# Hybrid diffusion trunk: weight splits emitted ahead in the scheduler's order, two steps of the RWKV units offered later to TensorE

## The chip, the cores and the metric

One core of a Trainium2 chip. The time is device microseconds of one execution of the program, the median of several runs; a profile of one execution stands beside it.

## What is computed

Two layers of one trunk over 512 latent tokens and 256 context tokens, 1024 wide, everything in 32-bit floats. Each layer is a half-step SwiGLU, token mixing, and another half-step SwiGLU, each behind a modulated RMS norm. Layer 0 mixes with eight heads of global attention beside eight heads of a bidirectional RWKV-7 recurrence; layer 1 with windowed attention.

```python
for l in range(DEPTH):
    x = x + 0.5 * m_lat[:, 2] * swiglu(modulate(rms_norm(x), m_lat[:, 0], m_lat[:, 1]), ffn_in[l, 0], ffn_out[l, 0])
    ctx = ctx + 0.5 * m_ctx[2] * swiglu(modulate(rms_norm(ctx), m_ctx[0], m_ctx[1]), ffn_in[l, 0], ffn_out[l, 0])
    ...
    o_lat, o_ctx = even_mixer(h_lat, h_ctx, ...) if l % 2 == 0 else odd_mixer(h_lat, h_ctx, ...)
    x = x + m_lat[:, 5] * o_lat
    x = x + 0.5 * m_lat[:, 8] * swiglu(modulate(rms_norm(x), m_lat[:, 6], m_lat[:, 7]), ffn_in[l, 1], ffn_out[l, 1])
    ...
return rms_norm(x, final_gain)

def step(S, inp):                     # the recurrence, one token, both directions
    r, w, k, v, kk, a = inp
    S = (S * w[:, :, None, :] - jnp.einsum('bhvk,bhk->bhv', S, kk)[..., None] * (kk * a)[:, :, None, :]
         + v[..., None] * k[:, :, None, :])
    return S, jnp.einsum('bhvk,bhk->bhv', S, r)
```

## The kernel before

**Dense products.** Each product with a weight is made in three matmuls of rounded 32-bit operands (`mm3`, L138 to L140): upper half of the weight times upper half of the activation (hi), upper times lower (lo), lower times upper. `weights` (L119 on) loads a 128x512 piece of a weight into `raw` by a DMA of SyncE (four buffers) and has `split` make `whi` on ScalarE (L116) and `wlo` on VectorE (L117), three buffers each. L138 and L139 read `whi`, L140 reads `wlo`. Four blocks of 128 columns come out of one piece. `d`, `g`, `c`, `y`, `s` are accumulation banks: two each of `d` and `g`, one of `c` and `y`, and one double bank `s` for attention.

**The even mixer** (some 600 to 1760 us) runs several generators merged into one order of TensorE. `dense` makes the projections of the context (256 columns a matmul) and of the latents (512), then the context's output product and its feed-forwards. `recurrence` is the chain of the RWKV units, twelve of them: four pairs of heads of the context (units 0 to 3), then four of the latents in two halves (4 to 11). `attention` makes the softmax tiles: scores L666, maximum L668 on VectorE, exponential L671 on ScalarE, transposes L610, values L624. `queued` takes what comes behind a projection: the norm of a query or key tile (`a_prepare2`, sums L380, reciprocal root by L333 on ScalarE and L334 on GpSimd, copy L389 on ScalarE, spread L392).

**What sets the order on TensorE.** `merge` (L175 on) keeps a clock in microseconds of TensorE. A generator yields a pair: how long its matmuls take, by which the clock goes on, and how long its next step's inputs take to be ready; it is offered again when the clock has passed 1.32 times the second number (L206). Of those offered the first in rank goes, or `dense` when it is owed a share (0.42, later 0.52 of the work). TensorE works through that order as it stands.

**What sets it on the other engines.** There a scheduler places the instructions by a priority, which is the place in the program less a boost. `merge` traces the steps of the recurrence under `high_priority(120)`; nothing else has a boost.

**A unit of the recurrence.** `rwkv_inverse` begins with sixteen matmuls for the four blocks of each direction d (L785): eight for d = 0 into two `g` banks, masked by two VectorE instructions (L787), then eight for d = 1 into two `g` banks again. Between the two stands a yield (L788). Later steps invert a triangular block in five levels (L822, L840). `rwkv_blocks` then goes through four blocks: L888 and L893 read the state, L899 multiplies by the inverse, VectorE (L900) and ScalarE (L901) copy the result, and L905 and L916 use it for the next state and the output; the yield between (L902) says 0.35 and 0.8.

Of the kernel before, what the change touches and what calls it, by code (L numbers as in the profile page):

```python
# [42 lines left out]
def flat(x):  # L43
    return x.rearrange("p a t -> p (a t)")
# [10 lines left out]
def fold(x):  # L55
    return x.rearrange("p (d t) -> p d t", d=2)
# [14 lines left out]
class Kernel:  # L71
# [47 lines left out]
    def weights(self, src, n, s):  # L119

        nc, pool = self.nc, s.wp
        out = []
        for c in range(0, n, 512):
            w = min(512, n - c)
            if self.early:
                raw = self.early.pop(0)
            else:
                raw = self.t(pool, [P, 512], "raw", bufs=4 if pool is self.wp else 3)
                nc.sync.dma_start(raw[:, :w], src[:, c : c + w])
            hi = self.t(pool, [P, 512], "whi", F32R, bufs=3)  # L130
            lo = self.t(pool, [P, 512], "wlo", F32R, bufs=3)
            self.split(raw[:, :w], hi[:, :w], lo[:, :w])
            out += [(hi[:, i : i + P], lo[:, i : i + P]) for i in range(0, w, P)]
        return out

# [39 lines left out]
    def merge(self, *gens, keep=None):  # L175


        gens += (keep,) if keep else ()
        self.parts, self.clock = [[rank, 0.0, gen] for rank, gen in enumerate(gens)], 0.0
        owed = 0.0  # L180
        with self.tc.manual_schedule(engines={mybir.EngineType.PE}):
            while self.parts:
                self.pause = keep is not None and len(self.parts) == 1
                ready = [p for p in self.parts if p[1] <= self.clock]
                if not ready:
                    self.clock = min(p[1] for p in self.parts)
                    continue
                p = min(ready, key=lambda p: p[0])
                if keep is not None and owed > 0:
                    p = next((q for q in ready if q[2] is keep), p)  # L190
                try:

                    with self.tc.high_priority(120) if p[2] in self.urgent else nullcontext():
                        step = next(p[2])
                except StopIteration:
                    self.parts.remove(p)
                    continue
                if step == "rest":
                    if len(self.parts) == 1:
                        break  # L200
                elif step is None:
                    p[1] = self.clock + 0.2
                else:
                    self.clock += step[0]
                    owed = min(owed + self.share * step[0], 2) - (step[0] if p[2] is keep else 0)
                    p[1] = self.clock + step[1] * 1.32  # L206
        self.parts, self.pause = None, False
# [562 lines left out]
    def rwkv_inverse(self, u):  # L770
# [9 lines left out]
        for d in (0, 1):  # L780
            mask = self.gmask[:, d].unsqueeze(1).to_broadcast([P, 4, P])
            pss = [self.bank("g") for _ in (0, 1)]
            for c in range(4):
                for e, q, _ in HALVES:
                    mm(pss[e][:, c * P : (c + 1) * P], flat(BK[q, 4 * d + c]), flat(A[q, 4 * d + c]), start=True, stop=True)  # L785
            for e, ps in enumerate(pss):
                tt(X[e][:, 4 * d : 4 * d + 4].rearrange("p c a t -> p c (a t)"), ps.rearrange("p (c n) -> p c n", n=P), mask, op=ALU.mult)  # L787
            yield 1.2, 0.6 * d  # L788


        ds = (slice(0, 4), slice(4, 8))
# [66 lines left out]
    def rwkv_blocks(self, u, S, Sout):  # L858


        nc, rp, W, A, X, PT, UV, tok = self.nc, self.rp, u.W, u.A, u.X, u.PT, u.UV, u.tok
        tt, mm, act = nc.vector.tensor_tensor, nc.tensor.matmul, nc.scalar.activation

        def decayed(s, n):

            if s is None:
                return None
            o = self.t(rp, [P, 2, 64], "SW", bufs=2)
            f, b = 64 + 66 * n, BS + 1 + 66 * (3 - n)
            nc.gpsimd.tensor_tensor(o, s, W[:, f : b + 1 : b - f].unsqueeze(2).to_broadcast([P, 2, 64]), op=ALU.mult)  # L870
            return o

        yb = self.bank("y")

        def y(d, c, q):
            return yb[q, c * 64 : c * 64 + 64]

        SW = decayed(S, 0)
        for n in range(4):
            pr = slice(n, 8 - n, 7 - 2 * n)  # L880
            bl = ((0, n), (1, 7 - n))
            cp = self.bank("c")
            if S is None:
                R = u.LV[:, pr]
            else:
                for d, c in bl:
                    for e, q, _ in HALVES:
                        mm(cp[q, 64 * d : 64 * d + 64], A[q, c, 0], S[q, d], start=True, stop=True)  # L888


                for d, c in bl:
                    for e, q, _ in HALVES:
                        mm(y(d, c, q), S[q, d], A[q, c, 1], start=n == d == 0, stop=False, skip_group_check=True)  # L893
                R = self.t(rp, [P, 2, 64], "R", bufs=2)
                tt(R, fold(cp[:, :128]), u.LV[:, pr], op=ALU.add)
                yield 0.75, 0.3
            for d, c in bl:
                for e, q, _ in HALVES:
                    mm(cp[q, 128 + 64 * d : 192 + 64 * d], PT[q, c], R[q, d], start=True, stop=True)  # L899
            nc.vector.tensor_copy(UV[:64, pr, 0], fold(cp[:64, 128:256]))  # L900
            act(UV[64:, pr, 1], fold(cp[64:, 128:256]), AF.Copy)  # L901
            yield 0.35, 0.8  # L902
            for d, c in bl:
                for e, q, _ in HALVES:
                    mm(cp[q, 256 + 64 * d : 320 + 64 * d], tok[:, c, e], UV[:, c, e], start=True, stop=True)  # L905
            Sn = Sout if n == 3 else self.t(rp, [P, 2, 64], "S", bufs=2)
            if Sn is not None:
                if SW is None:
                    nc.vector.tensor_copy(Sn, fold(cp[:, 256:384]))
                else:  # L910
                    tt(Sn, fold(cp[:, 256:384]), SW, op=ALU.add)
                if n < 3:
                    SW = decayed(Sn, n + 1)
            for d, c in bl:
                for e, q, _ in HALVES:
                    mm(y(d, c, q), UV[:, c, e], X[e][:, c, 1], start=S is None, stop=S is None or n == 3 and d == 1,  # L916
                       skip_group_check=S is not None)
            S = Sn
            yield 0.75, 0.2
        return yb  # L920
# [669 lines left out]
```

## Time and profile before

| what | before |
|---|---|
| median of 3 runs | 3248.78 us (3246.76 to 3249.76) |
| profiled execution, its own time | 3245.93 us |
| its span, first to last instruction | 3244.1 us |
| TensorE busy | 3072.4 us (95%) |
| VectorE busy | 2012.8 us (62%) |
| ScalarE busy | 1246.8 us (38%) |
| mean granted clock of TensorE | 0.981 |

Busy time of TensorE counts pipelined matmuls as they overlap, so a busy TensorE may still stream below its rate; a stall shows more plainly as idle time of the weight loads (PEld), each of which stands at the head of a matmul. The stages in order of time: first feed-forward of both streams to some 620 us, the even mixer to 1760, the feed-forwards of the latents with what is left of the context's work to 2500, the odd mixer to 2860, the last feed-forward.

### The profile page before, as it was taken

How to read it: one execution, taken by the hardware profiler on the slowest of the kernel's cores; microseconds unless marked ns; L12 is line 12 of the kernel's file. 1: busy time of each engine (PE TensorE's matmuls, PEld its weight loads, DVE VectorE, ACT ScalarE, POOL GpSimd, SP SyncE). 2: the span in 40 equal slices, each digit the busy share in tenths (PEclk: the TensorE clock that was granted, in tenths of full speed). 3: DMA queues.
4: the chain of work that ended last, by engine and by line, in shares of the span. 5: the costliest groups of instructions: out<-in, count | busy, mean ns of one | idle time of the engine just before them, and what ended most of it. 6: DMA issues, size and time to landing. Idle time of an engine off the chain costs nothing. (4 is left out here: it accounts for less than half of the span.)

```text
span 3244.1 us, 57779 instructions
## 1 busy us (share of the span) xinstructions
PE 3072.4 (95%) x22910; PEld 2623.1 (81%) x22910; DVE 2012.8 (62%) x3956; ACT 1246.8 (38%) x2595; POOL 303.7 (9%) x333
## 2 busy tenths in 40 slices
PE   5999999999997999999999999999999988999998
PEld 3888888887776789897888888888888867778887
DVE  7999973676665776767765444454344667754434
ACT  4222212544343444444444323343223456632322
POOL 3000000111124110102001000010000132010001
PEclk9999999999998999999999999999999999999999
DMA  6677672531111123332334333333333320023332
GB/s 229 206 215 216 211 257 61 169 101 58 43 43 54 33 88 99 95 100 74 101 128 134 107 96 97 96 116 97 97 96 95 113 75 24 27 81 97 96 97 88
DMA packets 174431, 349.59 MB, mean 108 GB/s; under 512 B 19408, under 2 KB 30544, under 8 KB 173776
## 3 DMA queue, kind: packets, MB, share of 16 engines
q1 hardware_dynamic: 169984, 340.86, 34.0%
q10 hardware_dynamic: 4176, 5.05, 0.5%
q8 instruction: 179, 2.93, 0.4%
q14 instruction: 92, 0.75, 0.1%
HBM read 340.59 MB, written 5.24 MB: 107 GB/s over the span
## 5 line engine op out<-in xcount | busy, mean ns | idle before, releaser
L116 ACT ACTIVATE whi<-raw 128x512 fp32r<-128x512 f32 (+1 forms) x996 | 615.4, 619 | 1359.5 <-PE d L139 502.0
L117 DVE TENSOR_TENSOR wlo<-raw,whi 128x512 fp32r<-128x512 f32 (+1 forms) x996 | 681.2, 686 | 683.3 <-ACT whi L116 667.2
L138 PE MATMUL d<-hL,whi 128*128 128x512 f32 x944 | 381.9, 405 | 3.2 <-ACT hL L404 2.6
L139 PE MATMUL d<-hL,whi 128*128 128x512 f32 x944 | 374.7, 397 | 2.3 <-DVE hL L405 2.2
L140 PE MATMUL d<-hL,wlo 128*128 128x512 f32 x944 | 371.9, 394 | 1.4 <-DVE wlo L117 1.4
L138 PE MATMUL d<-hC,whi 128*128 128x256 f32 x968 | 299.4, 309 | 7.6 <-ACT whi L116 4.5
L140 PE MATMUL d<-hC,wlo 128*128 128x256 f32 x968 | 278.4, 288 | 7.1 <-DVE wlo L117 6.7
L284 DVE SCALAR_TENSOR_TENSOR junk<-qL,cb 128x1024 bf16<-128x1024 f32 x224 | 273.3, 1220 | 11.6 <-DMA qL<-wmod 9.1
L139 PE MATMUL d<-hC,whi 128*128 128x256 f32 x968 | 277.2, 286 | 0.0
L140 PEld LDWEIGHTS d<-hL,wlo 128*128 128x128 f32 x944 | 179.8, 190 | 43.0 <-DVE wlo L117 2.6
L138 PEld LDWEIGHTS d<-hC,whi 128*128 128x128 f32 x968 | 188.5, 195 | 22.0 <-issue 6.9
L138 PEld LDWEIGHTS d<-hL,whi 128*128 128x128 f32 x944 | 180.3, 191 | 28.1 <-ACT hL L404 3.4
L139 PEld LDWEIGHTS d<-hL,whi 128*128 128x128 f32 x944 | 180.5, 191 | 24.2 <-DVE hL L405 3.6
L140 PEld LDWEIGHTS d<-hC,wlo 128*128 128x128 f32 x968 | 188.7, 195 | 10.2 <-DVE wlo L117 9.8
L139 PEld LDWEIGHTS d<-hC,whi 128*128 128x128 f32 x968 | 189.1, 195 | 0.5
L138 PE MATMUL d<-pL,whi 128*128 128x512 f32 x416 | 162.8, 391 | 0.0
L139 PE MATMUL d<-pL,whi 128*128 128x512 f32 x416 | 162.2, 390 | 0.0
L140 PE MATMUL d<-pL,wlo 128*128 128x512 f32 x416 | 162.0, 390 | 0.0
L138 PE MATMUL g<-hL,whi 128*128 128x512 f32 x384 | 149.4, 389 | 0.0
L139 PE MATMUL g<-hL,whi 128*128 128x512 f32 x384 | 149.4, 389 | 0.0
L140 PE MATMUL g<-hL,wlo 128*128 128x512 f32 x384 | 149.4, 389 | 0.0
L354 POOL TENSOR_TENSOR acc<-acc,sq 128x512 f32<-128x512 f32 x30 | 39.0, 1300 | 933.8 <-issue 710.6
(533 smaller groups left out, 6602.2 us busy)
## 6 DMA issues: line engine op xcount, KB each, us to landing
raw<-ffn_in SPq DMA_DIRECT2D x528, 256.0 KB, 2.9
qL<-wmod SPq DMA_DIRECT2D x132, 512.0 KB, 4.2
raw<-ffn_out SPq DMA_DIRECT2D x248, 256.0 KB, 2.7
raw<-even_in SPq DMA_DIRECT2D x84, 256.0 KB, 2.6
raw<-even_out SPq DMA_DIRECT2D x32, 256.0 KB, 2.6
raw<-odd_in SPq DMA_DIRECT2D x32, 256.0 KB, 2.8
raw<-ffn_out SPq DMA_DIRECT2D x56, 128.0 KB, 2.1
pL<-wmod SPq DMA_DIRECT2D x8, 512.0 KB, 8.8
```

The lines of the kernel that those rows point to most:

```text
L116: self.nc.scalar.activation(hi, src, AF.Copy)
L117: (eng or self.nc.vector).tensor_tensor(lo, src, hi.bitcast(F32), op=ALU.subtract)
L138: mm(out, w[0], mh, start=first, stop=False)
L139: mm(out, w[0], ml, start=False, stop=False)
L140: mm(out, w[1], mh, start=False, stop=last)
L284: nc.vector.scalar_tensor_tensor(self.t(self.fp, [P, D], "junk", bf), w, 0.5, self.cb[:, v], op0=ALU.mult, op1=ALU.mult, accum_out=out)
L354: eng.tensor_tensor(s.sq[0], s.sq[0], x, op=ALU.add)
```

## The change

Three things. The two instructions of each weight split are traced under a boost of 60, and the boost of the recurrence is raised from 120 to 160. The step of direction 1 in the first step of a unit is offered 1.2 x 1.32 us after the end of direction 0's matmuls, where it was offered at once. The step from L899 to L905 is offered 1.05 x 1.32 us after the clock where it was 0.8 x 1.32.

```diff
@@ weights
-            self.split(raw[:, :w], hi[:, :w], lo[:, :w])
+
+            with self.tc.high_priority(60):
+                self.split(raw[:, :w], hi[:, :w], lo[:, :w])
@@ merge
-                    with self.tc.high_priority(120) if p[2] in self.urgent else nullcontext():
+                    with self.tc.high_priority(160) if p[2] in self.urgent else nullcontext():
                         step = next(p[2])
@@ rwkv_inverse
-            yield 1.2, 0.6 * d
+
+            yield 1.2, 0.6 if d else 1.2
@@ rwkv_blocks
             act(UV[64:, pr, 1], fold(cp[64:, 128:256]), AF.Copy)
-            yield 0.35, 0.8
+            yield 0.35, 1.05
```

No instruction is added or removed. The lines of the changed kernel are two higher from the splits on (L138 is L140) and three higher behind L788 (L905 is L908).

TensorE, unit 0 (context), its first step; `pL` are the unit's own tiles, the rows of `hC` are dense matmuls. Before:

```order
L785 MATMUL g<-pL 128x128 x16
L138 MATMUL d<-hC,whi 128x256
L139 MATMUL d<-hC,whi 128x256
L140 MATMUL d<-hC,wlo 128x256
...
L806 MATMUL g<-ident,pL 64x64 x8
```

And now:

```order
L787 MATMUL g<-pL 128x128 x8
L140 MATMUL d<-hC,whi 128x256
L141 MATMUL d<-hC,whi 128x256
L142 MATMUL d<-hC,wlo 128x256
...
L787 MATMUL g<-pL 128x128 x8
```

The sixteen are parted in two eights, and 18 dense matmuls stand between them (three of these rows six times). Units 1, 4, 5 and 10 are parted in the same way.

TensorE, unit 0, its third and fourth block (L899 writes bank `c`, L905 needs the copy of it; `s` rows are the norm of a key tile). Before:

```order
L899 MATMUL c<-R,pL 64x64 x4
L905 MATMUL c<-pL 64x64 x4
L916 MATMUL y<-pL 64x64 x4
L392 MATMUL s<-ident,sq 128x128 x2
L888 MATMUL c<-S,pL 64x64 x4
L893 MATMUL y<-pL,S 64x64 x4
L899 MATMUL c<-R,pL 64x64 x4
L138 MATMUL d<-hC,whi 128x256
...
L905 MATMUL c<-pL 64x64 x4
```

And now, the end of the third block and the fourth:

```order
L382 MATMUL s<-bones,sq 128x2 x2
L908 MATMUL c<-pL 64x64 x4
L919 MATMUL y<-pL 64x64 x4
L140 MATMUL d<-hC,whi 128x256
...
L891 MATMUL c<-S,pL 64x64 x4
L896 MATMUL y<-pL,S 64x64 x4
L902 MATMUL c<-R,pL 64x64 x4
L394 MATMUL s<-ident,sq 128x128 x2
L908 MATMUL c<-pL 64x64 x4
```

The third block, bare before, now has twelve dense matmuls and a pair of sums ahead of L908; the fourth, which had twelve, has one transposing pair.

VectorE at the norm of the latents, beside the projections of the context (L403 and L405 modulate the latents, L685 and L686 shift a projected feature). Before:

```order
L117 TENSOR_TENSOR wlo<-raw,whi 128x512
L405 SCALAR_TENSOR_TENSOR hL<-pL,mod0L,hL 128x512
L685 SCALAR_TENSOR_TENSOR gC<-d,par,gC 128x255
L405 SCALAR_TENSOR_TENSOR hL<-pL,mod0L,hL 128x512
L686 SCALAR_TENSOR_TENSOR gC<-d,par,gC 128x255
L117 TENSOR_TENSOR wlo<-raw,whi 128x512
```

And now:

```order
L407 SCALAR_TENSOR_TENSOR hL<-pL,mod0L,hL 128x512
L117 TENSOR_TENSOR wlo<-raw,whi 128x512
L407 SCALAR_TENSOR_TENSOR hL<-pL,mod0L,hL 128x512
L117 TENSOR_TENSOR wlo<-raw,whi 128x512 x2
L687 SCALAR_TENSOR_TENSOR gC<-d,par,gC 128x255
L405 SCALAR_TENSOR_TENSOR pL<-qL,mod0L,s 128x512
L688 SCALAR_TENSOR_TENSOR gC<-d,par,gC 128x255
L117 TENSOR_TENSOR wlo<-raw,whi 128x512
```

Splits have moved ahead of modulations of the latents and of shifts of features.

## Rows read from the trace of the kernel before

**Rows 1.** The page's busy time: us, share of the span, instructions.

```profile
PE 3072.4 (95%) x22910; PEld 2623.1 (81%) x22910; DVE 2012.8 (62%) x3956; ACT 1246.8 (38%) x2595; POOL 303.7 (9%) x333
```

**Rows 2.** Windows: us; busy PE, PEld, DVE, ACT, POOL (count); granted clock, DMA, GB/s.

```profile
100.00:500.00 400.00, 398.84 (x2285) 349.92 (x2283) 369.83 (x682) 87.29 (x157) 0.00 (x0) 1.00 0.70 216
620.00:1000.00 380.00, 345.13 (x3674) 283.61 (x3672) 248.48 (x538) 166.32 (x393) 64.43 (x82) 0.97 0.23 72
1000.00:1020.00 20.00, 12.96 (x62) 10.22 (x62) 5.20 (x16) 4.53 (x14) 12.05 (x16) 0.57 0.00 0
1020.00:1760.00 740.00, 704.14 (x8603) 633.45 (x8604) 514.65 (x1062) 338.80 (x714) 102.52 (x111) 0.98 0.30 91
1760.00:2500.00 740.00, 736.31 (x3450) 618.18 (x3449) 333.44 (x513) 246.38 (x409) 8.77 (x7) 1.00 0.34 101
```

**Rows 3.** Waits of weight loads, 620 to 1760 us: total us, times, longest.

```profile
PEld s L610 <- ACT pr L671: 9.8, 11, 2.2
PEld d L140 <- DVE wlo L117: 8.5, 10, 2.0
```

**Rows 4.** Line L787 (masking), who waited for it: us, times.

```profile
  PEld g L785: 9.8, 14
```

**Rows 5.** Line L901 (copy), who waited for it: us, times.

```profile
  PEld c L905: 12.4, 17
```

**Rows 6.** Timeline at 1516 us: start, us, engine, line, operation [idle before].

```profile
1516.06 1.16 PE L785 MATMUL g<-hL 64*128 64x128 f32 x16
...
1517.69 1.28 DVE L787 TENSOR_TENSOR hL<-g,gmask 128x512 f32<-128x512 f32 x2
...
1518.42 1.75 PE L785 MATMUL g<-hL 64*128 64x128 f32 x16 [1.20 <-DVE hL L787]
```

**Rows 7.** Timeline at 1158 us, TensorE, behind eight covered matmuls of L785.

```profile
1158.16 0.38 PE L138 MATMUL d<-hC,whi 128*128 128x256 f32 x1
1158.38 0.28 PE L139 MATMUL d<-hC,whi 128*128 128x256 f32 x1
1158.50 0.28 PE L140 MATMUL d<-hC,wlo 128*128 128x256 f32 x1
```

**Rows 8.** Timeline at 1129 us, a block step without cover.

```profile
1128.79 0.45 PE L899 MATMUL c<-R,hL 64*64 64x64 f32 x8
...
1130.10 0.27 ACT L901 ACTIVATE hL<-c 64x128 f32<-64x128 f32 x1 [0.22 <-DVE hL L900]
1130.42 0.31 PEld L905 LDWEIGHTS c<-hL 128*64 128x64 f32 x8 [1.32 <-ACT hL L901]
```

**Rows 9.** Timeline at 648 us, a lower half behind a modulation.

```profile
647.66 0.74 DVE L405 SCALAR_TENSOR_TENSOR hL<-pL,mod0L,hL 128x512 fp32r<-128x512 f32 x1
...
648.16 0.28 PE L139 MATMUL d<-hC,whi 128*128 128x256 f32 x1
...
648.71 0.68 DVE L117 TENSOR_TENSOR wlo<-raw,whi 128x512 fp32r<-128x512 f32 x1
...
649.45 0.38 PE L140 MATMUL d<-hC,wlo 128*128 128x256 f32 x1 [1.01 <-DVE wlo L117]
```

**Rows 10.** The page's groups: count, busy us, mean ns, idle us before.

```profile
L116 ACT ACTIVATE whi<-raw 128x512 fp32r<-128x512 f32 (+1 forms) x996 | 615.4, 619 | 1359.5 <-PE d L139 502.0
L117 DVE TENSOR_TENSOR wlo<-raw,whi 128x512 fp32r<-128x512 f32 (+1 forms) x996 | 681.2, 686 | 683.3 <-ACT whi L116 667.2
```

**Rows 11.** Windows of 5 us in the first feed-forward, at either clock.

```profile
58.00:63.00 5.00, 4.89 (x16) 4.17 (x16) 5.00 (x13) 2.01 (x4) 0.00 (x0) 0.50 0.01 3
80.00:85.00 5.00, 5.00 (x30) 4.40 (x29) 3.86 (x10) 1.43 (x3) 0.00 (x0) 1.00 0.55 178
```

**Rows 12.** Waits of weight loads, 980 to 1020 us, the norms of query tiles.

```profile
PEld s L392 <- ACT sq L389: 5.1, 3, 2.1
```

**Rows 13.** Waits of weight loads, 625 to 655 us.

```profile
PEld d L140 <- DVE wlo L117: 4.1, 6, 1.2
```

## The prediction

> **What bounds the kernel now.** TensorE is busy for 3072.4 of 3244.1 us, VectorE for 2012.8 [rows 1], so the first question is where TensorE is not streaming. The windows by stage answer it [rows 2]: from 1760 to 2500 us it is busy for 736.31 of 740 at a granted clock of 1.00, and there a new order of the same matmuls cannot win anything. From 620 to 1760 us, the stage of the even mixer, it is busy for 345.13 + 12.96 + 704.14 = 1062.2 of 1140 us, so some 78 us are idle, and the clock is 0.97, 0.57 and 0.98. Nearly all that the change reorders on TensorE, and so nearly all that it can move, lies in these 1140 us; the number of instructions is the same on every engine.
>
> Then I read who is waited for there. A weight load stands at the head of each matmul and starts only when its data is there, so its idle time is the plainest measure of a stall. Three of the groups are what the three edits touch. The 64-row matmuls of the first step of an RWKV unit (L785) wait 9.8 us in 14 waits for the masking L787 [rows 4]. The state update of a block (L905) waits 12.4 us in 17 waits for the copy L901 [rows 5]. The third matmul of a split product (L140) waits 8.5 us in 10 waits for the lower half of a weight split, L117 [rows 3]. Together that is 30.7 us, under 1% of the span, and it bounds the direct gain.
>
> **The masking step, now offered later for direction 0.** Both directions need two banks "g", and there are two. Where their sixteen matmuls stand in one piece, the second eight wait until VectorE has masked both banks. In the unit at 1516 us the first eight end at 1516.06 + 1.16 = 1517.22, the two maskings end at 1517.69 + 1.28 = 1518.97, and the second eight begin only at 1518.42 and are stretched over 1.75 us instead of 1.16 [rows 6]. So a cover of about 1.75 us is wanted. The order shows what stands between now: in unit 0 nothing before, 18 matmuls of 256 columns after. One of these takes 0.12 us (1158.38 to 1158.50 [rows 7]), so the cover is 18 x 0.12 = 2.2 us, enough. Of twelve units five had no cover and two (units 2 and 3) one or two short matmuls; in the new order all but unit 3 have dense products or attention's matmuls between, and unit 3 keeps two short ones. I take 8.0 of the 9.8 us as saved and leave 1.8 for unit 3 and for maskings that are late for another reason. What is put between costs a change of operand shape: from the last L785 to the next dense pair the second start comes 0.22 us after the first instead of 0.12 [rows 7], so 0.1 us on the way in, the same out, and for seven units 7 x 0.2 = 1.4 us. Net -6.6; bounds -9.1 (all of the waits, half of the changes) and -3 (four of the seven covered too thinly).
>
> **The block step, offered 0.25 x 1.32 = 0.33 us later.** Between L899 and L905 lie the copies L900 and L901. At 1128.79 us L899 starts, L901 ends at 1130.10 + 0.27 = 1130.37, and L905 starts at 1130.42 after 1.32 us of idle weight load [rows 8]: without cover such a step costs about 1.3 us. The order has four bare steps of 48 before (0.7 us of matmuls or less), and two after, but these stand elsewhere: in unit 0 the third block gains its cover and the fourth loses it. The other waits come from copies that stand late in VectorE's or ScalarE's queue, and 17 waits x 0.25 us of added cover (the order's mean, 1.8 to 2.0 us by the 0.12 us above) is 4.2 at most. I take -3; bounds -6 and +1.5 (one more bare step).
>
> **The splits ahead.** Boosting them by 60 lifts them over vector work that was emitted up to 60 instructions earlier, while the recurrence keeps its lead of 100 (160 - 60). A split takes 0.686 us on VectorE and 0.619 on ScalarE [rows 10]. What there is to gain is seen at 648 us: the upper half is ready (L139 runs at 648.16), the lower half starts only at 648.71 after a modulation (L405) that the latents' norm needs later, and L140 comes at 649.45 [rows 9]. The window 625 to 655 us holds 4.1 of the 8.5 us, six of the ten waits [rows 13], and there the order does put splits ahead of L405. I take these and no more: -4; bounds -8.5 (every wait) and +1. That a split stands early in the queue while its slot is still taken, and holds up what is behind it, is not to be feared much: in the order a split comes behind the work whose matmuls precede the release of its slot. ScalarE already idles 502.0 us before the upper half because of L139 [rows 10], so most splits are bound by their slot, and the boost does nothing for them.
>
> **What these edits cost elsewhere.** First, attention. Each of its 48 softmax tiles (32 of the latents, 16 of the context) has a maximum on VectorE and an exponential on ScalarE, and they have no boost. L610 waits for that exponential 9.8 us in 11 waits already [rows 3]. If four more tiles find one more split ahead, at 0.65 us, that is +2.6. Second, the lean stretch around 1010 us, with TensorE busy for 12.96 of 20 us at a clock of 0.57 [rows 2]: dense products are held back there until the queue of the query tiles is empty, and the norms of these tiles run one after another through ScalarE, GpSimd and VectorE. The dense matmuls that now cover the RWKV steps were spent before it. In the order two stretches of 12 matmuls between those norms are gone. A bare step costs 5.1 / 3 = 1.7 us [rows 12]; two would be 3.4, but one more norm has been moved ahead of the lean stretch, so +2. Bounds of both together 0 and +9. The first feed-forward (100 to 500 us) is reordered on VectorE too, at no cost: TensorE is busy for 398.84 of 400 us there [rows 2], and the modulation sums that slip behind a split have until the end of that stage.
>
> **The clock.** [...] So the stage loses (1 - 0.97) x 380 + 0.43 x 20 + 0.02 x 740 = 35 us to the lower clock [rows 2], or 0.45 us for each of its 78 idle ones. Net of the costs, 6.6 + 3 + 4 - 4.6 = 9.0 us of waiting go; 9.0 x 0.45 = 4.0 come back with them. Bounds 0 and 8.
>
> The sum: -6.6 - 3 - 4 + 4.6 - 4.0 = -13.0. The profiled execution took 3245.93 us, so 3232.9; the median of the runs shown is 2.85 above it, which gives 3236 for a median.
>
> **The rivals.** *The waits only move* (3247). The same dense matmuls are spent on other steps, and whichever step they left is late instead. For it speaks the fourth block of unit 0 and the lean stretch; against it, that from 1020 us on TensorE is idle for only 36 of 740 us [rows 2], so dense work is not short there. Then the masking's 6.6 is eaten by bare steps, and only -2 remains: 3245.93 - 2 + 2.85.
> *The clock comes back* (3222). The low stretches are 35 us; if half of that returns in place of 4.0, the sum is -9.0 - 17.4 = -26.4. For it: the three windows with idle time are the three with a lower clock [rows 2]. Against: 8.6 of the 35 are the lean stretch, which stays.
> [...]
> *Attention behind the splits* (3265, slower). If half of the 48 softmax tiles find a split ahead on both engines, 24 x (0.69 + 0.62) = 31 us stand against 13.6 saved, with the 2.0 of the lean stretch and no clock gain: 3248.8 + 31 + 2 - 13.6 = 3268, less the few that still have cover, 3265. It outweighs the gain by 0.2% from about 14 tiles on. Against: only 11 of 48 wait at all now, and TensorE has cover between L666 and L610.
> [...]
> *The boost does nothing* (3238). The splits are bound by their slot, the term of -4 falls away and the attention's +2.6 with it; with 0.45 x 7.6 = 3.4 of clock the sum is -6.6 - 3 + 2 - 3.4 = -11.
>
> **How the numbers follow.** Forecast 3236: 0.46; waits move 0.22; clock 0.14; boost does nothing 0.10; attention 0.08. The forecast's own terms by their bounds span from 3221 (-9.1 - 6 - 8.5 with no cost and 4 of clock) to 3253 (-3 + 1.5 + 1 + 4.6 with no clock); that also takes in the rivals but the slow one and is my range. About 0.2%, 6.5 us, is what a measurement of this kernel can tell from no change. Below 3242.3 lie most of the forecast (0.43 of 0.46), the clock, and most of the boost's case (0.08): 0.65. Within 0.2%: the moved waits and the rest, 0.26. Slower: 0.09.
>
> **What would show it.** In the profile after, L787 should keep L785's weight loads waiting for under 3 us, L901 those of L905 for 8 to 10, L117 those of L140 for about 4; TensorE's busy time from 620 to the end of the mixer should be the same in about 12 us less; the L610 waits should be near 12 us. It is wrong if L610, L392 or L380 grow by as much as L785 shrinks (moved), if the clock in the stage rises above 0.99 (too small a gain foreseen), or if the span falls while these waits stand.

## The result, and the profile after

The changed kernel takes 3271.64 us (median of four runs, 3263.39 to 3274.0), the kernel before 3247.77 beside it on the same chip: a ratio of 1.0071, 95% interval 1.0058 to 1.0084. The prediction was 3236 us, faster. The profiled execution is the quickest of the four, 3263.39 us with a span of 3261.2 and a mean granted clock of 0.978. The other three take 8 to 11 us more at a mean clock of 0.975; 0.003 of 3270 us is some 10 us, about that difference, but no trace of them shows where it lies. So the profile below accounts for some 17 of the 24 us.

The page's busy time after, in us, share of the span, instructions ([rows 1] before):

```profile
PE 3074.0 (94%) x22910; PEld 2626.9 (81%) x22910; DVE 2010.7 (62%) x3956; ACT 1249.2 (38%) x2595; POOL 306.1 (9%) x333
```

The work is the same, the span 17 us longer. Windows after, columns as in [rows 2], the last two moved on by 16 us with the stage:

```profile
620.00:1000.00 380.00, 342.46 (x3671) 282.19 (x3669) 247.47 (x534) 166.04 (x391) 64.14 (x79) 0.97 0.23 73
1000.00:1020.00 20.00, 11.97 (x59) 9.64 (x60) 5.29 (x17) 3.29 (x10) 12.39 (x16) 0.54 0.02 6
1020.00:1776.00 756.00, 711.01 (x8635) 638.79 (x8631) 518.66 (x1072) 344.73 (x721) 104.59 (x113) 0.98 0.30 90
1776.00:2516.00 740.00, 737.31 (x3461) 621.03 (x3462) 331.07 (x510) 246.18 (x409) 9.79 (x8) 0.99 0.34 101
```

From 1020 us to the end of the mixer TensorE is idle for 45 us of 756, before for 36 of 740. Now the three waits that the edits were aimed at. Who waited for the masking (L789, was L787), for the copy (L904, was L901) and for the exponential (L673, was L671), each from its line's view; us, times:

```profile
  PEld g L809: 8.0, 7
  PEld g L787: 3.5, 2
...
  PEld c L908: 3.0, 5
...
  PEld s L612: 13.2, 13
```

Line L787 of the kernel before has, beside the row of [rows 4]:

```profile
  PEld g L806: 3.0, 3
```

The weight loads of L785 (now L787) wait 3.5 us for the masking where it was 9.8 [rows 4]. Those of the state update wait 3.0 where it was 12.4 [rows 5], and the third matmul of a `d` product no longer appears among those that wait for a lower half, 8.5 before [rows 3]. All three edits did what they say, the last two more than was forecast: 24 us of named waits are gone. But the next user of a `g` bank, L806 (now L809), which transposes the values into it and has to wait until the masking has emptied it, waits 8.0 us where it was 3.0, the softmax transposes 13.2 where it was 9.8, and other waits have grown. Weight loads over the mixer after, total us, times, longest:

```profile
PEld y L549 <- DVE pL L949: 9.1, 4, 2.8
...
PEld g L343 <- POOL rg L336: 5.3, 2, 3.0
PEld y L549 <- DVE y L1080: 4.4, 3, 2.2
...
PEld g L382 <- ACT xg L698: 3.4, 1, 3.4
```

and the same view of before:

```profile
PEld y L547 <- DVE pL L946: 6.1, 4, 2.7
...
PEld g L341 <- POOL rg L334: 3.8, 2, 3.0
```

L547 is the group sum in a unit's readout (`rwkv_read`, L925 on). A readout goes by halves of 256 columns through the one bank `y`: L945 is the last product of a half, L946 empties the bank, and the next L547 needs it. All its waits together are 9.4 us before and 16.2 after.

The idle time also comes in larger pieces. In the stretch that the table below calls the mixer, TensorE's traces have 10 gaps of over 1.5 us before, 23.6 us in all, and 19 after, 45.8 us; the shorter gaps fall from 57.0 us to 48.9.

To see where time is lost, the traces were lined up by work: matmuls are counted in order, each with the median interval of its shape in the kernel before, and one reads when each kernel has done the same amount. The mixer, from 551 to 1837 us before, takes 1285.8 us before and 1302.1 after; outside it the two differ by under 2 us in any stage. In the table "mixer" is that stretch against the kernel before, "idle" TensorE's idle time in it, "clock" the sum of (1 - granted clock) x time over windows of 8 us (the two overlap where TensorE idles at a low clock, as at 0.57 from 1000 to 1020 us [rows 2]), "readout" the waits of L547's weight loads for another instruction. All but the median and the ratio come from one execution. Up to 551 us executions differ by up to 5 us even where the order there is the same, so a span alone is no measure of a single profile. The mean clock of an execution varies too, for the kernel before from 0.983 (3243.87 us) to 0.978 (3253.11), so the last four columns carry some us of that.

| kernel | median us | ratio, 95% interval | mixer us | idle | clock | readout |
|---|---|---|---|---|---|---|
| before | 3247 | 1 | 0 (1285.8) | 80.6 | 32.3 | 9.4 |
| after | 3271.6 | 1.0058 to 1.0084 | +16.3 | 94.6 | 40.9 | 16.2 |
| e1 splits | 3262.6 | 1.0031 to 1.0057 | +17.1 | 88.0 | 44.2 | 12.9 |
| e2 both offers | 3263.8 | 1.0043 to 1.0068 | +9.3 | 84.6 | 44.3 | 14.2 |
| e3 masking | 3259.1 | 1.0029 to 1.0054 | +14.2 | 90.5 | 42.6 | 18.3 |
| e4 block | 3253.4 | 1.0014 to 1.0032 | +6.5 | 84.3 | 35.9 | 14.7 |
| e11 masking, latents | 3261.1 | 1.0034 to 1.0059 | +13.1 | 91.1 | 39.2 | 18.7 |
| e12 masking, context | 3246.2 | 0.9989 to 1.0006 | -2.5 | 80.9 | 30.6 | 9.2 |
| e15 masking, latents, 0.45 | 3246.2 | 0.9990 to 1.0008 | -1.1 | 85.3 | 25.6 | 10.1 |
| e18 block, 0.95 | 3248.0 | 0.9992 to 1.0010 | -0.4 | 81.2 | 30.6 | 9.3 |

### The profile page after: what moved, and what is told of

Its sections match the earlier page's. It is cut to its first block, busy times and chain, and to the rows that moved or that the text cites. A ratio compares the mean times of both kernels' runs of the same rounds, so it can differ in the third digit from the quotient of the medians.

```text
span 3261.2 us, 57820 instructions
## 1 busy us (share of the span) xinstructions
PE 3074.0 (94%) x22910; PEld 2626.9 (81%) x22910; DVE 2010.7 (62%) x3956; ACT 1249.2 (38%) x2595; POOL 306.1 (9%) x333
## 5 line engine op out<-in xcount | busy, mean ns | idle before, releaser
L140 PE MATMUL d<-hL,whi 128*128 128x512 f32 x944 | 382.8, 406 | 7.8 <-ACT hL L406 4.2
L140 PE MATMUL d<-hC,whi 128*128 128x256 f32 x968 | 301.7, 312 | 9.3 <-DVE gC L688 7.1
L140 PEld LDWEIGHTS d<-hC,whi 128*128 128x128 f32 x968 | 190.4, 197 | 24.5 <-issue 6.8
L140 PEld LDWEIGHTS d<-hL,whi 128*128 128x128 f32 x944 | 180.9, 192 | 33.9 <-ACT hL L406 5.8
L140 PE MATMUL d<-pL,whi 128*128 128x512 f32 x416 | 162.8, 391 | 0.0
L140 PE MATMUL g<-hL,whi 128*128 128x512 f32 x384 | 149.5, 389 | 2.0 <-ACT whi L116 2.0
```

The source lines that it names most:

```text
L140: mm(out, w[0], mh, start=first, stop=False)
```

## The experiments

**The change taken apart.** e1 has the boosts of the change, e2 its two offers, e3 and e4 one each of these.

```diff
 e1     with self.tc.high_priority(60): self.split(raw[:, :w], hi[:, :w], lo[:, :w])
 e1     high_priority(160) if p[2] in self.urgent   # 120 before
 e2 e3  yield 1.2, 0.6 if d else 1.2                # 0.6 * d before
 e2 e4  yield 0.35, 1.05                            # 0.35, 0.8 before
```

> The splits ahead alone (60 for the splits, 160 for the RWKV units), both offers as in the kernel before; the order of TensorE's matmuls is the old one but for a few dense ones after 2900 us, only VectorE's, ScalarE's and the load queue's orders change. Theory A (the splits hold up other vector work: softmax, features, norms, readouts): this alone is slower by 20 to 30 us, 3268 to 3278, with new waits of TensorE for L671, L686, L668 and L675. Theory B (the dense matmuls spent on the two RWKV steps are missing elsewhere): within 5 us of the kernel before, 3243 to 3253. Theory C (no part alone explains it, the parts disturb each other): between, +3 to +15.

> Both later offers alone (1.2 for direction 0 of the masking step, 1.05 for the block step), splits and units with the old priorities. Theory A: the gain that the prediction saw in them stands, 3234 to 3242 (-6.6 and -3 and some clock). Theory B: slower by 15 to 25 us, 3263 to 3273, with L785 and L905 waiting less and L610, L806, L624 or L392 more. Theory C: between, +3 to +15.

> Only the masking step's offer (1.2 for direction 0). The prediction's term: -6.6 and 3 of clock, 3238 to 3242; L787 keeps L785's weight loads waiting for under 3 us in place of 9.8. Theory B: L785's wait goes as well, but the time is +5 to +15 us. A result within 3 us of the kernel before means that the waits only move.

> Only the block step's offer (1.05). The prediction's term: -3 and 1.4 of clock, 3243 to 3245; L901 keeps L905 waiting for 8 to 10 us in place of 12.4. Theory B: +5 to +10 us, 3253 to 3258, with L905's waits down and others up.

Every part is slower by itself: +15.7, +16.9, +12.2 and +6.5 us by the medians. The three runs with an offer land where theory B wanted them (the dense matmuls are missing elsewhere), but theory A alone (it wanted a gain from the offers) and B alone (the splits harmless) both fail, and e1 at +15.7 is just above the +3 to +15 of C. In e3 no weight load of L785 waits for the masking any more, 9.8 us before [rows 4], and the kernel is 12 us slower. The parts do not add up: 15.7 + 16.9 = 32.6, against 24 for the whole.

**Who pays for the splits.** In e1 the order of TensorE's matmuls is that of before but for a few dense ones after 2900 us, so only the other engines' queues differ. Of its 17.1 us, 12.4 are lost in the first 250 us of the mixer, while the context's features are made and VectorE also has the modulations of the latents' norm; TensorE's idle time there goes from 19.5 to 26.1 us, and what the clock takes from 5.1 to 11.9. What TensorE waited for in this stretch, longest first, in e1 and then before (total, times, longest):

```profile
PE d L138 <- DVE gC L686: 6.3, 5, 3.5
PE s L610 <- ACT pr L671: 3.7, 2, 3.2
PE g L380 <- ACT xg L696: 3.2, 1, 3.2
...
PE d L138 <- DVE gC L686: 3.1, 2, 3.0
PE d L140 <- DVE wlo L117: 2.8, 4, 1.0
PE s L610 <- ACT pr L671: 2.5, 2, 2.0
```

A timeline of e1 there (start, us, engine, line, [idle before]):

```profile
640.15 0.45 ACT L684 ACTIVATE gC<-d,mu 128x256 f32<-128x256 f32 x1
640.43 0.69 DVE L117 TENSOR_TENSOR wlo<-raw,whi 128x512 fp32r<-128x512 f32 x1
640.96 0.63 ACT L116 ACTIVATE whi<-raw 128x512 fp32r<-128x512 f32 x1 [0.35 <-PE d L139]
641.62 0.69 DVE L117 TENSOR_TENSOR wlo<-raw,whi 128x512 fp32r<-128x512 f32 x1 [0.51 <-ACT whi L116]
642.23 0.48 DVE L685 SCALAR_TENSOR_TENSOR gC<-d,par,gC 128x255 f32<-128x255 f32 x1
642.63 0.74 DVE L403 SCALAR_TENSOR_TENSOR pL<-qL,mod0L,s 128x512 f32<-128x512 f32 x1
643.28 0.48 DVE L686 SCALAR_TENSOR_TENSOR gC<-d,par,gC 128x255 f32<-128x255 f32 x1
...
643.90 0.36 PE L138 MATMUL d<-hC,whi 128*128 128x256 f32 x1 [1.43 <-DVE gC L686]
```

A shift empties a dense bank in three steps, L684 on ScalarE and then L685 and L686 on VectorE. L684 is done at 640.60, but two lower halves stand ahead of L685 in VectorE's queue. For the second, VectorE stands idle for 0.51 us, since its upper half began only at 640.96: ScalarE had waited 0.35 us for the buffer, which L139 still read. So L685 starts at 642.23, L686 behind a modulation at 643.28, and TensorE, whose next product needs that bank, is idle for 1.43 us. VectorE's wait for upper halves before (551 to 1776 us), and after (551 to 1793; total, times, longest):

```profile
DVE wlo L117 <- ACT whi L116: 156.6, 142, 4.5
...
DVE wlo L117 <- ACT whi L116: 173.3, 156, 4.3
```

At 641 us VectorE held L685, whose input was there from 640.60 on, behind a split whose input came only at 641.59 (640.96 + 0.63).

In the change itself the same waits stand in this stretch (L686, now L688, 7.1 us; L696, now L698, 3.2), but other waits there are shorter, the clock takes 5.1 us as before, and the stretch loses only 1.5 us. The changed kernel's loss lies later: 11.5 of its 16.3 us behind the lean stretch, from 1025 us on.

e6 leaves the boost off in that stretch, e9 has it only there, e5 boosts the shifts too, e10 is e9 with shifts and the first unit's keys boosted:

```diff
 e6   with nullcontext() if context_features else high_priority(60): self.split(...)
 e9   with high_priority(60) if context_features else nullcontext(): self.split(...)
 e5   with high_priority(60): self.shifted(s, pt, c, x)          # beside e1
 e10  as e9, and in that stretch L684-L686, L694, L696 under high_priority(60)
```

> The splits ahead as in e1, and the feature shifts (L684 to L686) with the same boost of 60, so that a split passes only the norm's modulations and not the instructions that free a dense bank. Theory Q (VectorE works strictly in order and is full around 640 us, so a split put ahead delays the shift that TensorE needs next): the 12 us that e1 lost between 550 and 815 us go, and the time is 3243 to 3252. Theory R (the loss comes from elsewhere: splits standing in VectorE's queue before their upper half is there, over the whole mixer): 3258 to 3266, as e1.

> The splits ahead as in e1, but not while the context's features are made (some 600 to 690 us). Theory Q: all of e1's loss stands in that stretch, so 3244 to 3252. Theory R: most of the loss stays, 3256 to 3264.

> The complement of e6: the splits have the boost of 60 only while the context's features are made, and none elsewhere; TensorE's order is that of the kernel before, instruction for instruction. Theory Q (VectorE is full in this stretch and the splits push back what frees TensorE's banks): e1's 12 us between 550 and 815 us stand, 3254 to 3260, and e6 and this add up to e1. Theory S (any other order of VectorE's queue costs about the same, wherever): 3248 to 3254.

> As e9, with the feature shifts (L684 to L686) and the two instructions of the first unit's keys (L694, L696) under the same boost, so that only the norm's modulations (L403 to L405) stand behind; TensorE's order is again that of the kernel before. Theory Q: the stretch gains what the prediction saw in it, the 4.1 us of L140's waits, with nothing to pay, 3240 to 3246. Theory S: 3249 to 3256.

e6 takes 3253.9 us (ratio 1.0014 to 1.0033), between what Q and R wanted, and e9 3251.4 (1.0005 to 1.0023): +7 and +4.5, of e1's 15.7. So the stretch pays, but not alone, and e9 lies where theory S wanted it and not Q. e5 takes 3259.3 (1.0027 to 1.0055), not the 3243 to 3252 that theory Q wanted; of the 10.1 us that it loses in the first 250, the key sums L380 wait 5.6 us in one piece for L696, the next instruction without a boost. With that one lifted as well, e10 takes 3249.1 (1.0004 to 1.0022). Its trace, of the quickest of its eleven executions, loses 1.9 us in the stretch where e9's loses 5.8, but by the ratios e10 and e9 do not differ (1.0013 and 1.0014), e10 too lies where theory S wanted it, and the gain of 4 us that the prediction saw there is not to be measured. That whoever is left behind the splits pays can be seen in the traces; that lifting him as well wins the time back is not shown.

e17 asks that of the whole mixer:

```diff
+ high_priority(160 if p[2] in self.urgent else 60) for the recurrence and the generators it spawns
+ high_priority(60) for the splits and the feature shifts
```

> The splits ahead as in e1, with the feature shifts (60) and also the parts of the recurrence that are spawned as generators of their own (preparation, keys, readout, the context's blocks: 60; in the kernel before they have no boost, so in e1 the splits pass them). Behind the splits are left only the norm's modulations, attention and the norms of the query tiles. Theory Q for the whole mixer (what the splits pass on VectorE and ScalarE pays): e1's +16 shrinks to what attention and the tile norms pay, 3247 to 3254. If the loss is not in what is passed, it stays at 3258 to 3266.

It takes 3291.7 us (1.0127 to 1.0155), 45 us more than before, and no theory had that. What ScalarE waited for ahead of the exponential L671 there (21.5 us before), who waited for the exponential, and a wait of the scores L666 (us, times, of the last the longest):

```profile
  DVE st L669: 30.8, 26
...
  PEld s L610: 27.0, 13
...
PEld s L666 <- issue: 11.0, 3, 6.2
```

The readout, now ahead, waits only 6.7 us in all (9.4 before), the lower halves 4.1 (9.4), and the softmax transposes 27.0 where it was 9.8 [rows 3]. The scores wait 11.0 us for nothing that the profile shows, 0.7 before. TensorE's idle time in the mixer grows by 31 us, and 29 of them lie at these two lines. That is the rival "attention behind the splits" at a larger dose than the change has; how much of it is due to the splits and how much to the other lifted parts is not shown.

**Where the masking offer loses.** e11 makes the later offer for the eight units of the latents only, e12 for the four of the context.

```diff
 e11  yield 1.2, 0.6 if d else 1.2 * (u.s is self.L)
 e12  yield 1.2, 0.6 if d else 1.2 * (u.s is self.C)
 e15  yield 1.2, 0.6 if d else 0.45 * (u.s is self.L)
```

> The later masking offer for the eight units of the latents only (from 1030 us on). The prediction's count: the L785 waits of these units, about 6 us with the clock, go, 3241 to 3243. Theory P (the dense matmuls put between the halves are missing before the lean stretch at 1010 us): that stretch is untouched, so no loss, 3240 to 3248. Theory S: 3252 to 3260.

> The later masking offer for the four units of the context only (before 1010 us). Theory P: here is the loss, the lean stretch grows by 5 us and more, 3252 to 3260. The prediction's count: the 3 to 4 us of L785 waits of these units go and the lean stretch takes 2 of them back, 3244 to 3248. Theory S: 3250 to 3258.

All of e3's loss is in the latents (+14 us), which refutes theory P. The context is a case of a gain given back, and e12 lies in the 3244 to 3248 of the prediction's count. Windows that hold the same dense matmuls (1044, 254 and 128 before; 1045, 255 and 126 in e12): the context's units, then the stretch about the lean one, in the kernel before and in e12 (columns as in [rows 2]):

```profile
551.10:801.60 250.50, 231.02 (x2086) 201.32 (x2085) 167.78 (x330) 117.45 (x255) 34.60 (x38) 0.98 0.35 108
801.60:933.20 131.60, 123.91 (x1391) 94.84 (x1389) 88.85 (x202) 51.22 (x127) 18.06 (x23) 1.00 0.15 48
933.20:1025.40 92.20, 74.51 (x681) 60.58 (x681) 42.65 (x104) 36.98 (x95) 39.57 (x52) 0.83 0.13 39
...
555.70:801.00 245.30, 228.39 (x2055) 199.05 (x2054) 166.03 (x329) 117.72 (x253) 34.98 (x38) 0.99 0.36 110
801.00:929.30 128.30, 120.27 (x1316) 92.39 (x1315) 83.82 (x195) 50.86 (x126) 17.26 (x23) 1.00 0.16 49
929.30:1028.30 99.00, 79.23 (x787) 63.67 (x786) 46.54 (x114) 38.54 (x98) 40.98 (x52) 0.83 0.12 36
```

The first two are 8.5 us shorter together, the third 6.8 longer, since it now holds 106 more matmuls, none of them dense. So what was won went into dense products, done earlier, not into the recurrence: unit 3 begins at 918.9 us before and at 923.1 in e12, whose mixer begins 4.6 us later. TensorE's idle time falls from 19.5 to 16.9 us in the first window and rises from 17.7 to 19.8 in the third, where the tile norms leave it bare.

In the latents the place is the readout. A readout belongs to the unit just finished and is spawned as a generator of its own, without a boost. Its waits in e11 (weight loads, total, times, longest):

```profile
PEld y L547 <- DVE pL L946: 10.8, 4, 5.0
PEld y L547 <- DVE y L1077: 5.3, 4, 2.1
```

against 6.1 and 0.7 before. e4 shows such a place in full, TensorE and VectorE:

```profile
1172.98 0.70 PE L945 MATMUL y<-pL,g 128*128 128x256 f32 x2
1176.53 1.22 PE L547 MATMUL y<-y,bones 128*128 128x256 f32 x2 [2.85 <-DVE pL L946]
1177.67 2.08 PE L785 MATMUL g<-hL 64*128 64x128 f32 x16
...
1173.32 0.69 DVE L117 TENSOR_TENSOR wlo<-raw,whi 128x512 fp32r<-128x512 f32 x1
1173.92 1.28 DVE L787 TENSOR_TENSOR hL<-g,gmask 128x512 f32<-128x512 f32 x2
1175.12 0.90 DVE L797 COPY_PREDICATED hL<-pm,hL 64x256 f32<-64x256 uint8 x2
1176.05 0.42 DVE L946 TENSOR_TENSOR pL<-y 128x256 f32<-128x256 f32 x1
```

The next unit's first step has come to stand at the readout. Its masking and first inversion step (L787, L797: 2.18 us, boosted) go ahead of L946 on VectorE, and between L945 and L547 TensorE has no other matmul. It has none there before either, but then the gap at this place is short, and the masking comes only 3 us behind it:

```profile
1155.03 0.70 PE L547 MATMUL y<-y,bones 128*128 128x256 f32 x2 [0.90 <-DVE pL L946]
```

The clock falls behind the gap; windows of 3 us in e4:

```profile
1171.00:1174.00 3.00, 2.68 (x28) 1.91 (x24) 2.64 (x8) 0.80 (x2) 0.73 (x1) 1.00 0.28 87
1174.00:1177.00 3.00, 0.47 (x1) 0.48 (x2) 2.76 (x7) 0.00 (x0) 0.00 (x0) 0.78 0.28 87
1177.00:1180.00 3.00, 3.00 (x19) 2.13 (x19) 0.64 (x2) 0.42 (x1) 0.13 (x1) 0.50 0.00 0
1180.00:1183.00 3.00, 3.00 (x16) 2.79 (x17) 2.94 (x5) 0.52 (x1) 1.78 (x1) 0.58 0.00 0
```

TensorE was busy for 0.47 us of the second window; then the granted clock is 0.50, and the matmuls of L785 that follow take 2.08 us where a piece as long takes 1.16 [rows 6]. In the table above the readout stands at 14 to 19 us in every kernel with a full later offer in the latents, and at 9 to 10 in those that cost nothing. That the readout is the cause is read from such waits; no run changes the readout alone.

**Is it the offers, or any new order?** e7 moves the block step the other way; e8, e13 and e14 touch neither the splits nor the two steps by themselves; e15 and e18 are smaller doses of e11 and e4. Theory C of these expectations is not that of e1, but says that the loss goes with the dose of the offers.

```diff
 e7   yield 0.35, 0.3          (block step; 0.8 before)
 e8   self.share = 0.43        (0.42)
 e13  yield n / 1180, 0.2 + n / 350   (softmax tile; 0.4)
 e14  p[1] = self.clock + step[1] * 1.30   (1.32)
 e18  yield 0.35, 0.95         (block step)
```

> The block step's second number moved the other way, 0.8 to 0.3, so that the step is offered earlier; all else as before. Theory L (offering a step later holds up the recurrence, which is the chain that the mixer waits for): earlier is no loss, 3238 to 3248. Theory S (the order before is one of many with the same matmuls, and its neighbours are slower by 5 to 15 us whichever way they are reached): 3252 to 3262. By the prediction's own count, bare steps of 1.3 us at L905 come back: up to twice the 12.4 us of waits, 3250 to 3260.

> An edit that has nothing to do with the RWKV steps or the splits: the share of the work that the dense products are owed in the first part of the mixer is 0.43 in place of 0.42. It changes the order of TensorE's matmuls about as much as the masking edit did. Theory S: 3252 to 3262. Theory L: within 3 us of the kernel before, 3244 to 3250.

> An edit that touches neither the RWKV steps nor the splits: a softmax tile is offered again 0.26 us earlier (0.2 in place of 0.4 in its first yield). It reorders as many matmuls as the masking edit on the latents. Theory S (the neighbours of this order are slower by 4 to 15 us whichever way they are reached): 3251 to 3262. Theory C (the loss of e11 and e4 is particular to offering RWKV steps later, since the dense matmuls spent there are taken from steps that had them): within 4 us of the kernel before, 3243 to 3251.

> Every offer in the order of matmuls 1.5% earlier: the factor 1.32 is 1.30. No step is singled out, and the order differs in about as many places as with the masking edit. Theory S: 3251 to 3262. Theory C: within 4 us of the kernel before, 3243 to 3251.

> e11 with a smaller dose: direction 0 of the latents' masking step yields 0.45 in place of 0, not 1.2. Theory C: the loss goes with the cover that is spent, a third of e11's, 3249 to 3253. Theory S: no order in the dose, anywhere from 3248 to 3262. The prediction's count, where the three bare units of the latents are covered at little expense: 3241 to 3245.

> The block step's offer at 0.95 in place of 1.05 (0.8 before); the order of matmuls differs from the old one in a seventh as many rows. Theory C (the loss goes with the dose): within 3 us of the kernel before, 3244 to 3250. If any later offer costs as e4 does: 3251 to 3256.

e7: 3260.5 us (1.0026 to 1.0051); e8: 3251.0 (1.0003 to 1.0022); e13: 3251.4 (1.0005 to 1.0024); e14: 3250.7 (0.9997 to 1.0015); e15 and e18 as in the table, no different from before. The unrelated reorderings cost 2 to 5 us by their ratios, at the low end of theory S or under it, and the small doses nothing that can be measured, where theory C wanted a third of e11's loss for e15. So most of e11's 14 us is more than these reorderings cost; of e4's 6.5, with an interval that overlaps those of e8 and e13, that is not shown. A rival stays: the loss may go with the number of matmuls that stand elsewhere, whatever moved them. Counted in the traces, that is some 500 to 1400 of 22910 in e12, e15 and e18 (no loss), 2500 to 2800 in e8, e13 and e14 (2 to 5 us), 3700 in e11 and 4900 in e3 (14 and 12 us), 4100 in e7 (13 us); against it stands e4, 1400 for 6.5 us. Theory L falls. In e7 the last state update of the recurrence comes at 1651.5 us, 18.6 earlier than before (1670.1), and the kernel is 13 us slower; in e4 it comes 15 us later, and the kernel is 6.5 slower. The chain's end does not set the time. What the mixer pays in e7 is TensorE's bare places: it is 10.5 us longer, and TensorE's idle time is 10.5 us more. Only some of that is at L905 again (14.9 us of waits, 12.4 before [rows 5]).

**The harmless parts together.** e16 is e10 with e12.

> The two edits that cost next to nothing, together: e10 (splits, feature shifts and keys ahead of the norm's modulations while the context's features are made) and e12 (the later masking offer for the context's units). By their profiles, -2 and -2 in the mixer: 3242 to 3247. If what is won before the lean stretch at 1010 us is given back there, as in e12, it is 3245 to 3250.

3249.6 us (0.9999 to 1.0017): no gain. None of these kernels is faster than the one before.

## Why the prediction was wrong

*The waits it aimed at* were read rightly and even too cautiously. L785: -6.3 us against -8.0. L905: -9.4 against -3 (its "8 to 10 left" was 3.0). The lower halves: -8.5 against -4. What failed is the step from a wait to time: 24 us of these waits went, and TensorE's idle time in the mixer rose by 14.

*"From 1020 us on TensorE is idle for only 36 of 740 us, so dense work is not short there."* This is the step on which "the waits only move" was set aside, and it is false. Idle time that is low on average says that the cover is well spread, not that there is some to spare. With the later offer in the latents (e11) L785 and L806 together went from 12.8 to 11.8 us, L905 from 12.4 to 7.3, and the readout from 9.4 to 18.7, exponential and lower halves up by under 2 us each: 6 to 7 us more in all; the mixer is 13.1 us longer. In three of these eight units the masking stood bare before; the offer of 1.2 moved the others too, which had cover already. A dose of 0.45 (e15) costs nothing, and wins nothing.

*"The recurrence keeps its lead of 100."* That holds for the generator `chain` itself (`rwkv_inverse` and the latents' blocks). Preparation, keys, readout and the context's blocks are spawned, are not in `urgent`, and had no boost at all; the description of the kernel says too much there. The splits went ahead of them, as of the shifts that free a bank.

*"That a split stands early in the queue while its slot is still taken, and holds up what is behind it, is not to be feared much."* The rows at 641 us above show just that. The argument was from the order of matmuls, but the release comes at a time, and both engines stood until then, ScalarE for 0.35 us and VectorE for 0.51. The splits' term was -4; e1 measured +15.7, of which some 6 us are such waits (L686, 3.2 more, and L696, 3.2).

*The costs elsewhere* (+4.6, bounds 0 to +9) had attention nearly right in size: L610 went from 9.8 to 13.2, +3.4 where +2.6 was taken, and e1's part is 1.8 (11.6). The lean stretch had its size: TensorE's idle time about it is 2.1 us more in e12, against +2. The readout, +6.8, and L806, +5.0, were in no term. L806 needs a `g` bank that the masking of the second eight empties: to put these eight later is to bring their masking nearer to it. The upper end of the range took these costs at 4.6, not at their bound of 9, and the clock only as a gain.

*The clock* was -4.0 on the ground that idle time would fall. It rose, 80.6 to 94.6 us in the mixer, and the clock's loss with it: 32.3 to 40.9, and 44.2 in e1. So the sign followed the idle time there; but the 0.45 us for each idle one was the author's estimate, and no run shows it: in e7 and e15 the mixer has 10.5 and 4.7 us more of idle time than before, and loses 1.7 and 6.7 us less to the clock (30.6 and 25.6). What the trace shows of a low clock is the rate: 16 matmuls in 5 us at 0.50, 30 at 1.00 [rows 11].

*Where*: in the profiled execution all but 2 us of the loss lies in the mixer, as said; the feed-forwards paid nothing. Of the signs that the prediction named for "moved", L392 fell (6.4 to 3.1 us), L610 and L380 rose (by 3.4 and 4.0); the readout was not among them.

*The rivals.* "Attention behind the splits" (3265, chance 0.08) had the sign and nearly the time, but not the cause: attention carries a few us of it. "The waits only move" had the cause, and stopped at an even exchange; the exchange was at a loss: the waits that came were more, and in longer pieces, and the clock's loss in the mixer rose by 8.6 us.

*Open.* The parts' losses do not add up, and which waits are shared was not followed. In e11 the readout has 9 us more of waits, for a mixer 13 us longer; what the other waits give back and what the clock takes (7 us) overlap with it. Why the change loses 1.5 us in the stretch where e1 loses 12.4 was not followed. A boost of the readout alone beside the later offers was not tried.

## What to carry to other kernels

A list of waits on a chosen line is a list of places, not of prizes: before a step is given cover, name the step that has that cover now, and what its engine's queue holds at that moment. Move a step only where it is bare, and by no more than the cover it lacks; here the small doses cost nothing, though none of them won time. An instruction put ahead in a queue must be ready when its turn comes; in the rows at 641 us ScalarE waited 0.35 us for a buffer and VectorE then 0.51 for ScalarE, and what frees TensorE's bank waited with them.

## What was not expected of the hardware

One bare spot was paid for twice: 2.85 us of idle TensorE at the readout of e4, and then 6 us at a granted clock of 0.50 and 0.58, with 2.08 us for matmuls of L785 that take 1.16 in [rows 6]. The same stands behind a shorter gap. In the kernel before, the bare step of [rows 8] leaves TensorE idle for 1.19 us, and 1.3 us after its end comes (columns as in [rows 2])

```profile
1131.70:1134.70 3.00, 3.00 (x30) 2.43 (x30) 0.29 (x1) 0.74 (x2) 1.10 (x2) 0.50 0.00 0
```

It does not stand behind every gap: in the same trace TensorE is idle for 1.16 us ahead of L905 at 723.25 us and for 1.43 ahead of L785 at 1091.59, and the clock is 1.00 in the 6 us behind either; in the trace of after it is 1.00 in the 6 us behind 2.02 us of idle time that end at 1729.85.

Over the mixer the loss to the clock ranged from 25.6 us (e15) to 56.4 (e17), more than any single wait that the change was made for. Averaged over all executions on record, the mean clock is 0.978 for e1, 0.976 for e2 and 0.977 for e3, where the kernel before beside them has 0.981; 0.003 of 3250 us is some 10 us. It is not the whole loss: e7 has 0.981 as well and is 13 us slower.
